# Where operand tiles begin: padded and shifted SBUF tiles in a two-layer encoder trunk

## The chip, the core and the metric

The kernel runs on one NeuronCore of one Trainium2 chip. Five engines work side by side on instruction streams of their own: TensorE (PE in the profile, its weight loads PEld), VectorE (DVE), ScalarE (ACT), GpSimd (POOL) and SyncE (SP, which here issues nearly all DMAs). Operands lie in the on-chip memory SBUF, 128 partitions wide; matmul results go to the accumulators in PSUM. The metric is device time in microseconds (us) of one execution, lower is better.

## The reference

A trunk of two layers on x of 512 tokens x 1024 channels in fp32. Each layer has a token mixer and, beside it, a 4-head cross attention into 256 memory tokens. The mixer of layer 0 is differential attention, that of layer 1 a chunked gated linear attention (GLA). Then comes an output projection, and then a gated MLP with a causal convolution of width 3:

```python
for i in range(DEPTH):                      # DEPTH = 2
    h = rms_norm(x, attn_norm[i])
    proj = h @ w_in                         # (512, 1024) @ (1024, about 2560)
    mix = diff_attention(...) if i % 2 == 0 else gla_attention(...)
    cross = memory_cross_attention(mem_q, mem, ...)
    x = x + concatenate([mix, cross]) @ w_out[i]
    h = rms_norm(x, ffn_norm[i])
    x = x + conv_ffn(h, w_up[i], conv_w[i], conv_b[i], w_down[i])   # width 2816, twice
```

## The kernel before

The residual stream is held transposed: eight tiles xT[k] of 128 channels x 512 tokens. Every large product is made of three matmuls in the format fp32r, because one alone is not exact enough. An fp32 value v is split into a high part, v rounded to fp32r, and a low part, the rest; the product a*b is then ah*bh + ah*bl + al*bh. Helper `split` (L237) makes the pair of an activation: ScalarE writes the high part (L238), VectorE the low part (L239). `split_weights` (L200) does the same for weights (L201 and L204).

Three sorts of SBUF tiles matter here.

- The pool "xs" is a ring of 36 tiles with one tag, 128 partitions x 512 fp32, that is 2048 bytes of each partition. `xtile` (L146) takes one for plain data, `split_tiles` (L149) takes two for a pair of high and low part (names xsh and xsl).
- In the MLP, 5 of the products of each half are kept in xs pairs; the others are kept in a ring of 18 tiles of the same size, tag "mid" (names midh and midl). This ring lies in the pool of the MLP, behind rB, four tiles u of 514 columns each, and six tiles cvo.
- The pool "wp" holds weights: a ring of 3 raw tiles that the DMAs fill, and rings of 5 tiles each for the high and low part (whi and wlo), 1024 columns, 4096 bytes of a partition. One such tile holds a block of a piece of weights: 1024/w rows of 128 input channels, each w columns wide (w is 256, 512 or 272).

`gemm` (L244) makes the input projections: the activation block is the stationary operand, 128 x 128, and the weights are the moving one, up to 512 columns (L255 to L257). `product` (L267) makes the output projection and both MLP products the other way round: 128 columns of weights are stationary, and an activation tile of 512 tokens moves (L272 to L274):

```python
for i in ids:
    (hi, lo), (bh, bl) = parts[i], pairs[i]
    mm(p, hi[:, blk(n)], bh, start=i == first, stop=False)
    mm(p, hi[:, blk(n)], bl, start=False, stop=False)
    mm(p, lo[:, blk(n)], bh, start=False, stop=i == last)
```

The order of TensorE's work is written out by hand: a queue of small units (`Filler`) is drained between the steps of the attention by an estimated cost, so that projections fill the gaps. The other engines' order is set by the tile framework, which also puts in the waits. `weights` (L228) loads and splits the pieces of weights two ahead of their use, in the order of a fixed plan; the load is a DMA of 512 KB on SP's queue (L210).

In the MLP (`ffn`), L1026 to L1060 scale, convolve and gate the result of the up projection and split it again; `update` adds the down projection to xT (L978).

The constants (L161 to L164) lie in one tile C of 768 columns: the identity for transposes, two masks U and BEU in fp32, the same two masks read as integers (MP and MF), and a block of ones. Of the first two nothing reads U and BEU. Small scratch tiles of 16 columns have rings of four by `small` (L154).

Of the kernel before, what the change touches and what calls it, by code (L numbers as in the profile page):

```python
# [11 lines left out]
F32 = mybir.dt.float32  # L12
F32R = mybir.dt.float32r
I32 = mybir.dt.int32
# [7 lines left out]
S = 512  # L22
# [7 lines left out]
WTILE = 1024  # L30
HALVES = (6, 5)
XS = 36
WB = 5
# [96 lines left out]
def trunk(ctx, tc, head_d, x_t, mem_t, wpack, cols_a_d, cols_d, conv_d, gate_d, rel_bias, diff_lambda, consts, onehot, out):  # L130
# [4 lines left out]
    perm = ctx.enter_context(tc.tile_pool(name="perm", bufs=1))  # L135
    xs = ctx.enter_context(tc.tile_pool(name="xs", bufs=1))
    wp = ctx.enter_context(tc.tile_pool(name="wp", bufs=2))
# [5 lines left out]
    def bank(tag):  # L143
        return ps.tile([128, 512], F32, name=f"ps_{tag}", tag=tag)

    def xtile():  # L146
        return xs.tile([128, S], F32, name="xt", tag="xs", bufs=XS)

    def split_tiles(pool=None, tag="xs", bufs=XS):  # L149
        pool = pool or xs  # L150
        return (pool.tile([128, S], F32R, name=tag + "h", tag=tag, bufs=bufs),
                pool.tile([128, S], F32R, name=tag + "l", tag=tag, bufs=bufs))

    def small(name, bufs=None):  # L154
        return cp.tile([128, 16], F32, name=name, tag=name, bufs=bufs)

    def blk(b, w=128):
        return slice(w * b, w * b + w)


    C = perm.tile([128, 768], F32, name="C")  # L161
    ident, U, BEU = C[:, 0:128], C[:, 128:256], C[:, 256:384]
    MP, MF = C[:, 384:512].bitcast(I32), C[:, 512:640].bitcast(I32)
    ones = C[:, 640:768]  # L164
    eps = perm.tile([128, 1], F32, name="eps")
    V.memset(eps, EPS)

# [32 lines left out]
    def split_weights(c, raw, hi, lo, pin=False):  # L200
        ins = A.copy(hi[:, c], raw[:, c])  # L201
        if pin:
            tc.keep_in_program_order(ins)
        V.tensor_sub(lo[:, c], raw[:, c], hi[:, c].bitcast(F32))  # L204

    def raw_tile():
        return wp.tile([128, WTILE], F32, name="raw", tag="raw", bufs=3)

    def load_raw(raw, n):
        nc.sync.dma_start(raw[:, :n], wpack[at[0], :, :n])  # L210
        at[0] += 1
        return raw

    def make_piece(raws=None, between=None):
        parts = []
        for i, (_, _, kk, _, w) in enumerate(blocks[len(made)]):
            n = len(kk)
            raw = load_raw(raw_tile(), n * w) if raws is None else raws[i]
            hi, lo = (wp.tile([128, WTILE], F32R, name=t, tag=t, bufs=WB) for t in ("whi", "wlo"))
            if between is not None and i == 3:  # L220
                between()
            split_weights(slice(0, n * w), raw, hi, lo, len(made) == 2)
            parts += [(hi[:, blk(j, w)], lo[:, blk(j, w)]) for j in range(n)]
        made.append(parts)
# [12 lines left out]
    def split(hi, lo, src, gain):  # L237
        A.activation(hi, src, AF.Copy, scale=gain)  # L238
        V.scalar_tensor_tensor(lo, src, gain, hi.bitcast(F32), op0=ALU.mult, op1=ALU.subtract)  # L239
# [51 lines left out]
    def col(i, t=cols):  # L291
        return t[:, i:i + 1]
# [28 lines left out]
            V.tensor_copy(bs[c.start // 512], p[:6, :n])  # L321

    def lam(lv, lp):
        l2 = small("l2")[:, :2]
        lv4 = lv.rearrange("p (a c b) -> p a c b", a=2, c=2)
        V.tensor_mul(lp, lv4[:, :, 0], lv4[:, :, 1])
        V.reduce_sum(l2, lp, axis=AX.X)
        A.activation(l2, l2, AF.Exp)
        V.scalar_tensor_tensor(nlam, l2[:, 1:2], -LAM_INIT, l2[:, 0:1], op0=ALU.add, op1=ALU.subtract)
# [6 lines left out]
    def squares(src, acc):  # L336
        sq = xtile()
        A.activation(sq, src, AF.Square)
        if acc[0] is not None:
            V.tensor_add(sq, sq, acc[0])  # L340
        acc[0] = sq
# [16 lines left out]
    load = nc.sync.dma_start  # L358
    with tc.tile_pool(name="ini", bufs=1) as ip, tc.manual_schedule(engines={E.Activation, E.DVE, E.Pool, E.SP}):
        idle = ip.tile([128, 512], F32, name="idle")  # L360
        rb = ip.tile([32, 6], F32, name="rb")
        oh = ip.tile([32, 640], F32, name="oh")
        bs = xtile()[:6], xtile()[:6, :128]
        lv = xtile()[:, :256]
        G.memset(idle, 0.0)
        p = bank("tp")
        for n in (512, 320):
            mm(p[:, :n], idle[:, 0:128], idle[:, :n], start=True, stop=True)


        raws = [ip.tile([128, WTILE], F32, name=f"raw{i}") for i in range(4)]
        A.dma_start(raws[0][:, blk(0, S)], wpack[0, :, blk(0, S)])
        head = ip.tile([128, 32 + S], F32, name="head")
        for c in (slice(0, 32 + S // 2), slice(32 + S // 2, 32 + S)):
            load(head[:, c], head_d[:, c])
        xT[0] = head[:, 32:]
        for k in range(1, KT):
            xT[k] = xtile()
            load(xT[k], x_t[k])
            load(raws[k // 2][:, blk(k % 2, S)], wpack[k // 2, :, blk(k % 2, S)])  # L380
        load(cols_a, cols_a_d)
        at[0] = 4
        load(C[:, 640:768], consts[:, 640:768])
        load(rb, rel_bias)
        load(oh, onehot)
        second = [load_raw(raw_tile(), WTILE) for _ in range(3)]
        load(cols, cols_d)
        load(lv, diff_lambda[0].rearrange("a b -> (a b)").partition_broadcast(128))
        parts, acc, split_w = [], [None], [None]
        made.append(parts)  # L390

        def operands(k):
            if k % 2 == 0:
                split_w[0] = [wp.tile([128, WTILE], F32R, name=n, tag=n, bufs=WB) for n in ("whi", "wlo")]
            c = blk(k % 2, S)
            hi, lo = split_w[0]
            xh[k], xl[k] = split_tiles()
            if k == 0:
                V.tensor_copy(hi[:, c], raws[0][:, c])
                V.tensor_sub(lo[:, c], raws[0][:, c], hi[:, c].bitcast(F32))  # L400
                for t in (blk(0, S // 2), blk(1, S // 2)):
                    split(xh[0][:, t], xl[0][:, t], xT[0][:, t], col(0, head))
            else:
                split(xh[k], xl[k], xT[k], col(k, head))
                split_weights(c, raws[k // 2], hi, lo)
            parts.append((hi[:, c], lo[:, c]))
            squares(xT[k], acc)

        operands(0)
        for k in range(KT):  # L410
            if k + 1 < KT:
                operands(k + 1)
            if k == 0:
                second.append(load_raw(raws[0], WTILE))
            if k == 4:
                bias_rows(rb, oh, bs)
            if k == KT - 2:
                make_piece(second, lambda: token_rsqrt("lg", acc[0], NB, r_x[:, 0]))
                weights(("qk", 0))
                small_vectors()  # L420
                for c in range(2):
                    load(bias_d[:, 512 * c:min(512 * c + 512, 640)], bs[c])
            hi, lo = parts[k]
            terms = (xh[k], hi), (xh[k], lo), (xl[k], hi)
            todo = [(b, i) for b in range(NB) for i in range(3)]
            for b, i in sorted(todo, key=lambda bi: bi[1]) if k == 0 else todo:
                xp, w = terms[i]
                mm(first[b], xp[:, blk(b)], w, start=k == 0 and i == 0, stop=k == KT - 1 and i == 2)

    load(C[:, 0:640], consts[:, 0:640])  # L430
    for i in range(4):
        load(memT[i], mem_t[i])
    for l in range(2):
# [294 lines left out]
    def gla_layer(pool, mix, acc):  # L728
# [6 lines left out]
        gl = pool.tile([128, NB, 16], F32, name="gl", bufs=1)  # L735
        gl3, gw3 = split_tiles()
        gl3, gw3 = gl3[:96], gw3[:96, :384]
        rq, rh = small("rq"), small("rh")

        def scales():  # L740
            token_rsqrt("sm", acc[0], NB, r_x[:, 2], True)
# [58 lines left out]
        for h in range(4):  # L800
            pz = bank(("lg", "sm")[h % 2])
            mm(pz[:96], gw3[:, blk(h, 96)], gl3, start=True, stop=True)
            t, la = xtile()[:96], xtile()[:96]
# [291 lines left out]
def _constants():  # L1095
    import numpy as np

    i = np.arange(128)
    same = (i[:, None] // 64) == (i[None, :] // 64)
    le = i[:, None] <= i[None, :]  # L1100
    c = np.zeros((128, 768), np.float32)
    c[:, 0:128] = np.eye(128)
    c[:, 128:256] = same & le
    c[:, 256:384] = same & ~le
    c[:, 384:512] = same & le
    c[:, 512:640] = same & ~le
    c[:, 640:768] = 1.0

    rel = np.arange(640) - 511
    n = np.abs(rel)  # L1110
    large = 8 + sum((n >= t).astype(np.int64) for t in (12, 16, 23, 32, 46, 64, 91))
    bucket = np.where(n < 8, n, large) + np.where(rel > 0, 16, 0)
    onehot = (np.arange(32)[:, None] == bucket[None, :]).astype(np.float32)
    return c, np.ascontiguousarray(onehot[:, ::-1])
# [53 lines left out]
```

## Time and profile before

| | |
|---|---|
| median of 3 runs | 1196.5 us (1195.61 to 1196.85) |
| the profiled execution | 1194.47 us, its span 1192.7 us |
| PE busy | 1179.3 us, 5656 instructions |
| PEld busy | 965.8 us |
| DVE busy | 760.1 us |
| ACT busy | 548.3 us |
| DMA | 117.81 MB, mean 99 GB/s |
| granted TensorE clock | 1.000 |

A row of the timeline gives the start of an instruction (us from the start of the span), how long it was in flight, engine, line, operation, output <- inputs, shape, and, in brackets, the idle time before it. Matmuls are pipelined: each is in flight for longer than the distance from its start to the start of the next, and the end is modelled. The distance of the starts is the cost of a matmul in a dense run, and is called the step here. In the groups, "x96 | 38.0, 396 | 0.0" is the count, the busy time in us, the mean of one in ns, and the idle time before them. A line of the waits gives who waited for whom, the total in us, how often, and the longest.

### The profile page before, as it was taken

Reading aid. Unit: us, or ns where it says so; the run is one execution under the profiler, and the core shown is the slowest. Engines: PE = TensorE matmul, PEld = TensorE weight load, DVE = VectorE, ACT = ScalarE, POOL = GpSimd, SP = SyncE. Lnnn points to the kernel's source line nnn. Section 1 sums busy time; section 2 is a strip of 40 time slices with the busy share of each in tenths; the row PEclk is TensorE's granted clock in tenths of the full one; section 3 lists DMA queues with packets and bytes.
Section 4 is the critical chain, followed back from the end, with each engine's and each line's share of the span. In section 5 each row is a group of like instructions: output and inputs, shape, how many; then the busy total and the mean of one; then the engine's idle time right before and its main releaser. Section 6 shows DMA issues by size and latency. Waiting matters only on the chain.

```text
span 1192.7 us, 14774 instructions
## 1 busy us (share of the span) xinstructions
PE 1179.3 (99%) x5656; PEld 965.8 (81%) x5656; DVE 760.1 (64%) x1270; ACT 548.3 (46%) x966; POOL 4.5 (0%) x25
## 2 busy tenths in 40 slices
PE   9999998999999999999999999999999999999998
PEld 6887776788888888888888788987888888888887
DVE  7566587687767434767556746768777743476741
ACT  6676586564434223434436534436443422243420
POOL 0000000000000000000000000000000000000000
PEclk9999999999999999999999999999999999999999
DMA  8322214042322332322342221333233233242231
GB/s 296 124 96 81 80 55 141 27 136 76 116 96 86 109 107 71 123 71 89 117 144 78 72 71 58 103 104 125 73 109 103 81 114 106 71 124 72 89 115 44
DMA packets 39268, 117.81 MB, mean 99 GB/s; under 512 B 4671, under 2 KB 6520, under 8 KB 39198
## 3 DMA queue, kind: packets, MB, share of 16 engines
q1 hardware_dynamic: 39054, 116.62, 30.5%
q8 instruction: 44, 0.72, 0.3%
q10 hardware_dynamic: 144, 0.26, 0.1%
q14 instruction: 26, 0.21, 0.1%
HBM read 112.65 MB, written 4.21 MB: 98 GB/s over the span
## 4 chain that ended last, share of the span: by engine, by line
PE 93%; DVE 3%; ACT 2%; DMA 1%; issue 1%; SPq 0%; ACTq 0%; DVEq 0%
PE ps_mm L273 8%; PE ps_mm L274 8%; PE ps_mm L272 8%; PE ps_sm L274 7%; PE ps_sm L273 7%; PE ps_sm L272 7%; PE ps_mm L255 5%; PE ps_mm L257 5%; PE ps_mm L256 5%; PE ps_lg L273 3%; PE ps_lg L272 3%; PE ps_lg L274 3%; PE ps_tp L272 3%; PE ps_tp L273 3%; PE ps_tp L274 3%; PE ps_tp L170 2%
## 5 line engine op out<-in xcount | busy, mean ns | idle before, releaser
L201 ACT CAST whi<-raw 128x1024 fp32r<-128x1024 f32 (+4 forms) x212 | 208.5, 985 | 263.9 <-PE ps_tp L273 134.7
L204 DVE TENSOR_TENSOR wlo<-raw,whi 128x1024 fp32r<-128x1024 f32 (+4 forms) x212 | 241.3, 1140 | 117.1 <-ACT whi L201 116.4
L272 PE MATMUL ps_mm<-xsh,whi 128*128 128x512 f32 x446 | 176.4, 396 | 0.0
L273 PE MATMUL ps_mm<-xsl,whi 128*128 128x512 f32 x446 | 173.8, 390 | 0.2 <-DVE xsl L239 0.2
L274 PE MATMUL ps_mm<-xsh,wlo 128*128 128x512 f32 x446 | 173.7, 389 | 0.0
L272 PE MATMUL ps_sm<-xsh,whi 128*128 128x512 f32 x386 | 150.3, 389 | 0.0
L274 PE MATMUL ps_sm<-xsh,wlo 128*128 128x512 f32 x386 | 150.2, 389 | 0.0
L273 PE MATMUL ps_sm<-xsl,whi 128*128 128x512 f32 x386 | 150.2, 389 | 0.0
L255 PE MATMUL ps_mm<-whi,xsh 128*128 128x512 f32 (+2 forms) x352 | 136.9, 389 | 0.1
L257 PE MATMUL ps_mm<-whi,xsl 128*128 128x512 f32 (+2 forms) x352 | 131.1, 373 | 0.3 <-DVE xsl L239 0.3
L256 PE MATMUL ps_mm<-wlo,xsh 128*128 128x512 f32 (+2 forms) x352 | 130.6, 371 | 0.0
L1028 ACT ACTIVATE cvo<-u,cv 128x512 f32<-128x512 f32 x88 | 71.6, 814 | 121.4 <-DVE u L1026 121.4
L273 PEld LDWEIGHTS ps_mm<-xsl,whi 128*128 128x128 f32 x446 | 83.8, 188 | 17.8 <-DVE xsl L239 0.6
L272 PEld LDWEIGHTS ps_mm<-xsh,whi 128*128 128x128 f32 x446 | 83.8, 188 | 17.5 <-issue 0.8
L274 PEld LDWEIGHTS ps_mm<-xsh,wlo 128*128 128x128 f32 x446 | 83.7, 188 | 17.4
L1029 DVE SCALAR_TENSOR_TENSOR cvo<-u,cv,cvo 128x512 f32<-128x512 f32 x88 | 65.8, 748 | 38.7 <-ACT cvo L1028 38.7
L273 PEld LDWEIGHTS ps_sm<-xsl,whi 128*128 128x128 f32 x386 | 72.5, 188 | 15.1
L272 PEld LDWEIGHTS ps_sm<-xsh,whi 128*128 128x128 f32 x386 | 72.5, 188 | 15.0
L274 PEld LDWEIGHTS ps_sm<-xsh,wlo 128*128 128x128 f32 x386 | 72.5, 188 | 15.0
L255 PEld LDWEIGHTS ps_mm<-whi,xsh 128*128 128x128 f32 x352 | 66.3, 188 | 13.8 <-issue 3.4
L257 PEld LDWEIGHTS ps_mm<-whi,xsl 128*128 128x128 f32 x352 | 66.1, 188 | 12.6 <-DVE xsl L239 0.5
L256 PEld LDWEIGHTS ps_mm<-wlo,xsh 128*128 128x128 f32 x352 | 66.4, 189 | 9.7
(257 smaller groups left out, 1734.9 us busy)
## 6 DMA issues: line engine op xcount, KB each, us to landing
raw<-in_wpack_dram SPq DMA_DIRECT2D x178, 512.0 KB, 3.5
xt<-in_x_t_dram SPq DMA_DIRECT2D x15, 256.0 KB, 5.9
raw<-in_wpack_dram SPq DMA_DIRECT2D x15, 256.0 KB, 2.6
raw<-in_wpack_dram SPq DMA_DIRECT2D x8, 384.0 KB, 3.4
xres<-xt SPq DMA_DIRECT2D x8, 256.0 KB, 2.0
xt<-xres SPq DMA_DIRECT2D x8, 256.0 KB, 3.9
out_dram<-xt SPq DMA_DIRECT2D x8, 256.0 KB, 2.0
bt<-bias_d SPq DMA_DIRECT2D x6, 256.0 KB, 3.1
```

The costliest lines, as they stand in the source:

```text
L170: nc.tensor.transpose(dst, src, ident[:n, :n])
L201: ins = A.copy(hi[:, c], raw[:, c])
L204: V.tensor_sub(lo[:, c], raw[:, c], hi[:, c].bitcast(F32))
L255: mm(p, sh[k][:, blk(b)], hi, start=k == 0, stop=False)
L256: mm(p, sh[k][:, blk(b)], lo, start=False, stop=False)
L257: mm(p, sl[k][:, blk(b)], hi, start=False, stop=k == KT - 1)
L272: mm(p, hi[:, blk(n)], bh, start=i == first, stop=False)
L273: mm(p, hi[:, blk(n)], bl, start=False, stop=False)
L274: mm(p, lo[:, blk(n)], bh, start=False, stop=i == last)
L1028: A.activation(c, u[:, 2:], AF.Identity, scale=cv[l][:, 2, j:j + 1], bias=cv[l][:, 3, j:j + 1])
L1029: V.scalar_tensor_tensor(c, u[:, 1:S + 1], cv[l][:, 1, j:j + 1], c, op0=ALU.mult, op1=ALU.add)
```

## The change

The tiles of xs, of mid and of the split weights become longer than what is used of them: 528 columns for 512, and 1032 for 1024. A pair of split tiles is in addition used from column 0, 4, 8 or 12 on, in turn (0, 16, 32 or 48 bytes). Plain x tiles are used from column 0. So the places where the tiles begin, which were all the same modulo 512 bytes within a pool, now differ from tile to tile in steps of 16 bytes. Two unread masks are dropped from the constants, and three small scratch tiles get one buffer instead of four, which makes room for the padding. What is computed, and the order in which PE computes it, stay the same.

```diff
     def xtile():
-        return xs.tile([128, S], F32, name="xt", tag="xs", bufs=XS)
+        return xs.tile([128, S + 16], F32, name="xt", tag="xs", bufs=XS)[:, :S]
+
+    shift = cycle((0, 4, 8, 12))
 
     def split_tiles(pool=None, tag="xs", bufs=XS):
-        pool = pool or xs
-        return (pool.tile([128, S], F32R, name=tag + "h", tag=tag, bufs=bufs),
-                pool.tile([128, S], F32R, name=tag + "l", tag=tag, bufs=bufs))
+        pool, o = pool or xs, next(shift)
+        return (pool.tile([128, S + 16], F32R, name=tag + "h", tag=tag, bufs=bufs)[:, o:o + S],
+                pool.tile([128, S + 16], F32R, name=tag + "l", tag=tag, bufs=bufs)[:, o:o + S])
...
-    C = perm.tile([128, 768], F32, name="C")
-    ident, U, BEU = C[:, 0:128], C[:, 128:256], C[:, 256:384]
-    MP, MF = C[:, 384:512].bitcast(I32), C[:, 512:640].bitcast(I32)
-    ones = C[:, 640:768]
+    C = perm.tile([128, 512], F32, name="C")
+    ident = C[:, 0:128]
+    MP, MF = C[:, 128:256].bitcast(I32), C[:, 256:384].bitcast(I32)
+    ones = C[:, 384:512]
...
-            hi, lo = (wp.tile([128, WTILE], F32R, name=t, tag=t, bufs=WB) for t in ("whi", "wlo"))
+            hi, lo = (wp.tile([128, WTILE + 8], F32R, name=t, tag=t, bufs=WB)[:, :WTILE] for t in ("whi", "wlo"))
...
-        l2 = small("l2")[:, :2]
+        l2 = small("l2", 1)[:, :2]
...
-                split_w[0] = [wp.tile([128, WTILE], F32R, name=n, tag=n, bufs=WB) for n in ("whi", "wlo")]
+                split_w[0] = [wp.tile([128, WTILE + 8], F32R, name=n, tag=n, bufs=WB)[:, :WTILE] for n in ("whi", "wlo")]
...
-    load(C[:, 0:640], consts[:, 0:640])
+    load(C[:, 0:384], consts[:, 0:384])
...
-        rq, rh = small("rq"), small("rh")
+        rq, rh = small("rq", 1), small("rh", 1)
```

More of the change, by code (lines that the diff above doesn't have):

```diff
@@ L382, in trunk @@
         at[0] = 4
-        load(C[:, 640:768], consts[:, 640:768])
+        load(C[:, 384:512], consts[:, 384:512])
         load(rb, rel_bias)
@@ L1100, in _constants @@
     le = i[:, None] <= i[None, :]
-    c = np.zeros((128, 768), np.float32)
+    c = np.zeros((128, 512), np.float32)
     c[:, 0:128] = np.eye(128)
@@ L1104, in _constants @@
     c[:, 256:384] = same & ~le
-    c[:, 384:512] = same & le
-    c[:, 512:640] = same & ~le
-    c[:, 640:768] = 1.0
+    c[:, 384:512] = 1.0
     rel = np.arange(640) - 511
```

## The prediction

> **What bounds the kernel now.** I read the page first, top down: TensorE (PE) has work in flight for 99% of the span, in every slice, at the full granted clock, and the chain that ended last is 93% PE. The other engines have room.
>
> ```profile
> span 1192.7 us, 14774 instructions
> PE 1179.3 (99%) x5656; PEld 965.8 (81%) x5656; DVE 760.1 (64%) x1270; ACT 548.3 (46%) x966; POOL 4.5 (0%) x25
> PEclk9999999999999999999999999999999999999999
> PE 93%; DVE 3%; ACT 2%; DMA 1%; issue 1%; SPq 0%; ACTq 0%; DVEq 0%
> ```
>
> Next the waits of PE. The longest is 2.2 us; all that are listed come to about 9 us, so there is no wait whose removal or lengthening would be the main term.
>
> ```profile
> PE ps_sm L640 <- DVE o L649: 2.2, 1, 2.2
> PE ps_lg L504 <- DVE nmd L609: 1.3, 1, 1.3
> PE ps_lg L604 <- ACT xt L511: 1.1, 3, 0.5
> ```
>
> So the time is the number of matmuls times the time from the start of one to the start of the next, and that step is what I looked for in the timeline. These rows are PE's in the first down projection of layer 0: the first and the last of 24 matmuls whose moving operand is an xsh or xsl tile, then the first ones and the last of 21 with a midh or midl tile, then xsh again.
>
> ```profile
> 388.81 0.39 PE L272 MATMUL ps_sm<-xsh,whi 128*128 128x512 f32 x1
> ...
> 394.02 0.39 PE L274 MATMUL ps_lg<-xsh,wlo 128*128 128x512 f32 x1
> 394.25 0.40 PE L272 MATMUL ps_lg<-midh,whi 128*128 128x512 f32 x1
> 394.48 0.39 PE L273 MATMUL ps_lg<-midl,whi 128*128 128x512 f32 x1
> 394.70 0.40 PE L274 MATMUL ps_lg<-midh,wlo 128*128 128x512 f32 x1
> 394.94 0.39 PE L272 MATMUL ps_lg<-midh,whi 128*128 128x512 f32 x1
> 395.17 0.40 PE L273 MATMUL ps_lg<-midl,whi 128*128 128x512 f32 x1
> ...
> 398.90 0.40 PE L274 MATMUL ps_lg<-midh,wlo 128*128 128x512 f32 x1
> 399.14 0.39 PE L272 MATMUL ps_tp<-xsh,whi 128*128 128x512 f32 x1
> ```
>
> With xs tiles the step is (394.25 - 388.81)/24 = 226.7 ns. With mid tiles it is (399.14 - 394.25)/21 = 232.9 ns, 6.2 ns more, for the same shape, the same weight tiles and the same engine. The groups by form say it over the whole kernel: 395 to 396 ns in flight against 389 to 391.
>
> ```profile
> L273 PE MATMUL ps_lg<-midl,whi 128*128 128x512 f32 x96 | 38.0, 396 | 0.0
> L274 PE MATMUL ps_tp<-midh,wlo 128*128 128x512 f32 x96 | 38.0, 395 | 0.0
> L273 PE MATMUL ps_lg<-xsl,whi 128*128 128x512 f32 x80 | 31.3, 391 | 0.0
> L274 PE MATMUL ps_lg<-xsh,wlo 128*128 128x512 f32 x80 | 31.1, 389 | 0.0
> L274 PE MATMUL ps_sm<-xsh,wlo 128*128 128x512 f32 x386 | 150.2, 389 | 0.0
> ```
>
> What differs is where the tiles begin. In the addresses of the built program every xs, whi and wlo tile begins at 416 modulo 512 bytes, since their sizes (2048 and 4096 bytes) are multiples of 512 and the blocks of weights used within them start 512 bytes apart. The mid tiles lie behind four u tiles of 514 elements (2056 bytes, taking 2080), so they begin 4 x 32 = 128 bytes further on, at 32. While one matmul streams its moving operand, the weights of the next are loaded. I call the distance between these two starts, modulo 512, the phase. Of the 4515 matmuls with 512 fp32r columns, 3931 have phase 0 before the change and 576, those on mid tiles, have phase 128; 8 have others. So the trace already holds a small trial of the change, and there a start out of phase is dearer.
>
> A second sample speaks more mildly. The projection "gm" of layer 1 packs blocks of 272 columns (1088 bytes), so its moving blocks run through phases 0, 64 and 128. From 630.27 to 636.17 there are 47 of them.
>
> ```profile
> 630.27 0.29 PE L256 MATMUL ps_mm<-wlo,xsh 128*128 128x272 f32 x1
> ...
> 636.17 0.40 PE L255 MATMUL ps_mm<-whi,xsh 128*128 128x512 f32 x1
> ```
>
> ```profile
> 760.47 0.28 PE L255 MATMUL ps_mm<-whi,xsh 128*128 128x256 f32 x1
> ...
> 762.50 0.28 PE L257 MATMUL ps_mm<-whi,xsl 128*128 128x256 f32 x1
> ```
>
> The 17 matmuls of 256 columns from 760.47 to 762.50, all in phase, take 119.4 ns each, 120 within the rounding. Against 226.7 ns for 512 columns that is 0.417 ns a column and a fixed 13.3 ns. 272 columns in phase should then take 126.7 ns; the mix of three phases took 5.90/47 = 125.5 ns. So a phase of 64, and 128 on a shorter block, cost nothing there.
>
> **The change part by part.** *Tiles that begin elsewhere.* xs tiles get 528 columns for 512 (a pitch of 2112 bytes, 64 more), mid tiles likewise, each pair of split tiles starts 0, 4, 8 or 12 elements into its tile, and whi and wlo get 1032 columns for 1024 (32 bytes more). In the addresses of the changed program the phases of the same 4515 matmuls spread over all 32 steps of 16 bytes: 92 at 0, 1048 within 64 bytes of 0 on either side, 3467 further out. Before, 584 were further out. No instruction is added, and PE's order is the same in both programs.
>
> The price of a phase that no row shows is bounded by the rows there are. Below: the 272-column mix, -1.2 ns; below even that, nothing excludes that the whole fixed 13.3 ns is a collision at phase 0 and goes. Above: the longest mid matmuls are in flight for 398 ns against 389, 9 ns more, and I let the fixed part double (+13.3 ns) as the outer end, since a half-turn of 256 bytes is in no row.
>
> ```profile
> L272 PE MATMUL ps_lg<-midh,whi x96: 392/395/398, 394.2 to 1181.2; 128*128 128x512 f32 x96
> ```
>
> I take 6.2 ns for a phase beyond 64 bytes, as the mid rows are the only ones of the same shape, 4515 such matmuls being nearly the whole of PE (4515 x 0.2267 = 1024 us of 1192.7), and nothing within 64 bytes, as the 272-column rows show. (3467 - 584) x 6.2 ns = 17.9 us. All of it is on the path: PE is the chain, and there is no idle time on it to take it in. The ends are -3839 x 13.3 ns = -51 us and +51 us for the 3839 matmuls that leave phase 0; by the nearest rows -3839 x 1.2 = -4.6 us and +3839 x 9 = +34.6 us.
>
> By the Trainium skill, "TensorE: Matmul & The Clock Gate", section "Step-by-step: what each phase is for", TensorE has two independent SBUF read ports, one for the streaming operand and one for LDWEIGHTS. By that the two streams would not meet and this term would be 0. The trace does not agree: 232.9 against 226.7 ns with nothing else changed. It stands below as a rival.
>
> *VectorE and ScalarE on the same tiles.* They read and write the moved tiles. L1060 does the same subtraction into mid tiles (32) and xs tiles (416):
>
> ```profile
> L1060 DVE TENSOR_TENSOR midl<-cvo,midh x24: 683/692/693, 331.4 to 1139.1; 128x512 fp32r<-128x512 f32 x24
> L1060 DVE TENSOR_TENSOR xsl<-cvo,xsh x20: 682/685/693, 279.1 to 1086.5; 128x512 fp32r<-128x512 f32 x20
> ```
>
> The medians differ by 1%. Taken over VectorE's 760 us it would be 7 us on an engine that is idle for 36%, under PE's work: 0. Where that cover is thin, at the splits that PE waits for, it is 7 ns each. The range takes it in.
>
> *Smaller constants and shorter rings of small tiles.* The load of C shrinks from 640 to 384 columns (320 to 192 KB), the doubled masks U and BEU go, MP and MF move within C; l2, rq and rh get one buffer where each is made once. Nobody in PE's list of waits waits for C, and a DMA moved past the gate loads on SP's queue changes no listed wait: 0. If C's arrival did hold the first transposes, the gain would be under 1 us.
>
> ```profile
> C<-in_consts_dram SPq DMA_DIRECT2D x1, 320.0 KB
> ```
>
> *DMAs of the moved tiles.* Each partition still gets one run of 2048 bytes; the transfers that refill xs tiles land in 3.9 us and are asked for well before their use. The last store (2.0 us) is on the path and starts at a 32-byte multiple as before: 0, at most some tenths of a us.
>
> ```profile
> xt<-xres SPq DMA_DIRECT2D x8, 256.0 KB, 3.9
> out_dram<-xt SPq DMA_DIRECT2D x8, 256.0 KB, 2.0
> ```
>
> **The sum.** The profiled execution took 1194.5 us (span 1192.7 and 1.8 around it), 2.0 below the median of 1196.5. 1194.5 + 17.9 = 1212.4, and on the scale of the median 1214.4. I say 1214.
>
> **The rivals.** *Faster: phase 0 is itself the collision.* All tiles at one place mean that the moving stream and the weight load go through the same part of each 512 bytes in step, and the fixed 13.3 ns may be what that costs. Spread phases would then lose less on the mean. For it: the 272-column mix is 1.2 ns under what phase 0 gives, and one mid matmul took only 0.22 us (394.48 to 394.70). Against it: the mid tiles as a whole. By the 272-column price it is 1196.5 - 4.6 = 1192; with a quarter of the fixed part gone, 3839 x 3.3 ns = 12.8 us, 1184; with all of it, 1145. It decides from the point where the mean over the phases falls under the 226.7 ns of phase 0.
>
> *No change: the places don't matter.* The mid matmuls would be slow for another cause of their own place in the memory, not for the phase, or the gains of some phases pay for the losses of others. 1196.5. This is also where the two read ports of the skill's page lead. Against it: the step returns to 0.23 us and under as soon as xs tiles are back, and all other loads of the stage are the same.
>
> *Much slower: jumps cost more than a fixed phase.* Mid tiles keep one phase from matmul to matmul; after the change nearly every matmul starts at another. If each of 3839 then pays the 9 ns of the slow mid matmuls, 1196.5 + 34.6 = 1231; at double the fixed part, 1248. For it: the few matmuls after the return to xs tiles are still slow (0.40 us in the row below, 0.39 in phase).
>
> ```profile
> 399.37 0.40 PE L273 MATMUL ps_tp<-xsl,whi 128*128 128x512 f32 x1
> 399.84 0.40 PE L272 MATMUL ps_tp<-xsh,whi 128*128 128x512 f32 x1
> ```
>
> **How the numbers follow.** A measurement of this kernel tells a difference from about 0.2% (2.4 us) on. Slower by a price near that of the mid rows, 1203 to 1226: 0.48. Much slower: 0.19. Faster: 0.27, of which some 0.08 below 1182. No change: 0.06. So slower 0.67, same 0.06, faster 0.27. The range leaves out what lies over 1240 (0.08) and under 1182 (0.08). The likeliest case alone is 1203 to 1226.
>
> **What would show it.** Right: the groups of 512-column matmuls on xs tiles rise from 389 to about 394 ns, the step from 226.7 to 231 ns or so, evenly in all stages and not in one; PE's waits stay as short as they are; VectorE's and ScalarE's means stay within 1%. The runs on mid tiles, whose phases now vary as well, would no longer stand out against their neighbours. Wrong: a mean under 389 ns on xs tiles (phase 0 was the collision), or PE waits for DVE or ACT that grow by more than 2 us in all (the moved tiles slow the other engines), or a difference of time with an unchanged step.

## The result, and the profile after

The changed kernel takes 1210.7 us (median of 4 runs, 1209.6 to 1212.1) against 1196.7 us before: 14.0 us more, ratio 1.0126 with a 95% interval of 1.0113 to 1.0138. The forecast was 1214, slower with a chance of 0.67.

The page of the profiled execution after the change; its span of 1210.3 us belongs to a run of 1212.1 us, so the spans differ by 17.6 us where the medians differ by 14.0. The second line is busy time by engine, the last the chain that ended last.

```profile
span 1210.3 us, 14771 instructions
PE 1196.6 (99%) x5656; PEld 968.0 (80%) x5656; DVE 760.7 (63%) x1270; ACT 547.5 (45%) x966; POOL 4.5 (0%) x25
PEclk9999999999999999999999999999999999999999
PE 90%; DVE 4%; ACT 3%; DMA 2%; issue 1%; SPq 0%; ACTq 0%; DVEq 0%
```

The same 5656 records keep TensorE busy for 17.3 us longer, at the same clock; VectorE and ScalarE do their work in the same time as before (760.7 and 547.5 us against 760.1 and 548.3). The waits of PE are the same ones; of what is new, the longest is 0.4 us:

```profile
PE ps_sm L642 <- DVE o L651: 2.2, 1, 2.2
PE ps_lg L506 <- DVE nmd L611: 1.3, 1, 1.3
PE ps_mm L257 <- ACT ks L559: 0.4, 1, 0.4
```

The groups by form after the change, columns as in the prediction (the lines have moved by 2):

```profile
L275 PE MATMUL ps_lg<-midl,whi 128*128 128x512 f32 x96 | 38.0, 396 | 0.0
L276 PE MATMUL ps_sm<-xsh,wlo 128*128 128x512 f32 x386 | 151.9, 394 | 0.0
```

Every group of 512 columns with an xs tile as its moving operand has gained 2 to 6 ns in flight, the one shown from 389 to 394; the mid groups have stayed or lost up to 2 ns, and no longer stand out. The timeline of the same down projection gives the step: 41 matmuls on xs tiles from 392.66 to 402.13 us take 231.0 ns each (226.7 before), the 15 on mid tiles from there to 405.61 take 232.0 (232.9 before).

```profile
392.66 0.39 PE L275 MATMUL ps_sm<-xsl,whi 128*128 128x512 f32 x1
...
402.13 0.40 PE L274 MATMUL ps_lg<-midh,whi 128*128 128x512 f32 x1
...
405.61 0.39 PE L274 MATMUL ps_lg<-midh,whi 128*128 128x512 f32 x1
```

So nothing waits for longer; it is the matmuls that have become a little slower. The distances from one start to the next, added up over both traces, say where the time went: behind the projections' 960 matmuls of 512 columns 228.2 us before and 232.3 after, behind the products on xs tiles 679.7 and 693.9, on mid tiles 134.6 and 133.6, behind all others 144.8 and 145.0. That is 17.3 us for the large matmuls and 0.2 us for the rest.

### The profile page after: what moved, and what is told of

The parts are those of the page before. It is cut to its first block, busy times and chain, and to the rows that moved or that the text cites. A ratio compares the mean times of both kernels' runs of the same rounds, so it can differ in the third digit from the quotient of the medians.

```text
span 1210.3 us, 14771 instructions
## 1 busy us (share of the span) xinstructions
PE 1196.6 (99%) x5656; PEld 968.0 (80%) x5656; DVE 760.7 (63%) x1270; ACT 547.5 (45%) x966; POOL 4.5 (0%) x25
## 4 chain that ended last, share of the span: by engine, by line
PE 90%; DVE 4%; ACT 3%; DMA 2%; issue 1%; SPq 0%; ACTq 0%; DVEq 0%
PE ps_mm L275 8%; PE ps_mm L276 8%; PE ps_mm L274 8%; PE ps_sm L274 7%; PE ps_sm L276 7%; PE ps_sm L275 7%; PE ps_mm L257 5%; PE ps_mm L259 5%; PE ps_mm L258 5%; PE ps_lg L275 3%; PE ps_lg L276 3%; PE ps_lg L274 3%; PE ps_tp L274 3%; PE ps_tp L275 3%; PE ps_tp L276 3%; PE ps_tp L172 2%
```

## The experiments

Three explanations were open. The phase theory: the step depends on where the moving operand begins against the weights. The hop theory: a constant place costs little, but a place that changes from matmul to matmul does. And: it is other engines, or the place in the memory, that make matmuls slow.

### The matmuls alone, phase by phase

```python
for a, b, n in steps:      # a: start of the moving operand, b: of the weights, n: columns
    nc.tensor.matmul(p[i % 4][:, :n], st[:, b:b + 128], mv[:, a:a + n], start=True, stop=True)
    i += 1
```

> The kernel's work is left out: nothing but fp32r matmuls on one 128x2048 moving and one 128x1024 stationary tile, in runs of 36 or 72, with no other engine at work, so that TensorE's own two streams are alone. Runs paa to pdh hold one phase each (start of the moving operand less start of the weights that are being loaded, modulo 512 bytes), from 0 to 496 bytes in steps of 16. ba and bb move both operands by 128 and 256 bytes (phase 0), ca and cb the weights alone. da hops to another phase with every matmul, db, dc and dd change between 0 and 128, 256 and 64 bytes, de hops in steps of 64, df hops with the weights in steps of 32. ea and eb repeat one pair of operands at phase 0 and 128. ga to gd are 256 and 384 columns at 0 and 128. Phase theory: 226.7 ns at 0, 233 at 128 (run pba), other phases between 224 and 238, ba and bb 226.7, ca and cb as the phases 384 and 256. Hop theory: every steady phase is near 226.7, and da, de are at 231 to 232. If the mid tiles were slow for their place in the memory or for other engines, all runs are at 226.7.

In the timeline of PE equal instructions are merged, so each run of matmuls is a row, and the distance of two starts over 36 (or 72) is the mean step. Runs pab to pbh are the phases 16 to 240, pca to pch the phases 256 to 368.

```profile
20.18 8.50 PE L61 MATMUL pab<-mv,st 128*128 128x512 f32 x36
28.51 8.57 PE L61 MATMUL pac<-mv,st 128*128 128x512 f32 x36
36.92 8.55 PE L61 MATMUL pad<-mv,st 128*128 128x512 f32 x36
...
78.61 8.53 PE L61 MATMUL pba<-mv,st 128*128 128x512 f32 x36
86.97 8.55 PE L61 MATMUL pbb<-mv,st 128*128 128x512 f32 x36
...
137.42 8.33 PE L61 MATMUL pbh<-mv,st 128*128 128x512 f32 x36
145.58 8.36 PE L61 MATMUL pca<-mv,st 128*128 128x512 f32 x36
153.78 8.50 PE L61 MATMUL pcb<-mv,st 128*128 128x512 f32 x36
162.12 8.57 PE L61 MATMUL pcc<-mv,st 128*128 128x512 f32 x36
...
279.19 8.38 PE L61 MATMUL ba<-mv,st 128*128 128x512 f32 x36
287.40 8.33 PE L61 MATMUL bb<-mv,st 128*128 128x512 f32 x36
295.57 8.53 PE L61 MATMUL ca<-mv,st 128*128 128x512 f32 x36
303.94 8.32 PE L61 MATMUL cb<-mv,st 128*128 128x512 f32 x36
312.10 16.88 PE L61 MATMUL da<-mv,st 128*128 128x512 f32 x72
328.81 16.72 PE L61 MATMUL db<-mv,st 128*128 128x512 f32 x72
345.38 16.50 PE L61 MATMUL dc<-mv,st 128*128 128x512 f32 x72
361.72 16.80 PE L61 MATMUL dd<-mv,st 128*128 128x512 f32 x72
```

From these rows: 231.4 ns at phase 16, 233.6 at 32, 232.2 at 128 (pba); rows left out here give 229.2 at 64 and 234.2 at 160. At 240 (that is -16) it is 226.7, as good as in phase. At 256 it is (153.78 - 145.58)/36 = 227.8, with the run's first matmuls still slow; then the curve repeats: 231.7 at 272 against 231.4 at 16. The period is 256 bytes and not 512. From 145.58 to 279.19, one whole turn of 256 bytes, 576 matmuls take 232.0 ns each. Moving both operands costs nothing (bb: 226.9), moving the weights alone costs the same as moving the other operand (ca: 232.5, cb by 256: 226.7). Hops over all phases give 232.1 (da), hops of 0 and 256 bytes 226.9 (dc). So hops over all phases cost what constant phases cost on the mean, and nothing more. Hops between 0 and 64 bytes do cost more: 231.0 (dd, with the start of the run after it), where the mean of the two phases is 228.0. TensorE does all this to itself, as no other engine was at work. No phase is clearly below 226.7 ns.

### The mid ring in phase

```diff
-        us = [pool.tile([128, S + 2], F32, name=f"u{i}", bufs=1) for i in range(4)]
+        us = [pool.tile([128, S + 26], F32, name=f"u{i}", bufs=1)[:, :S + 2] for i in range(4)]
```

> The kernel before with the four u tiles padded to 538 columns, so that the mid ring begins 4 x 128 bytes later and is at 416 modulo 512 like all other operands. Phase theory: the mid groups fall from 395 to about 390 ns in flight, the step from 232.9 to 226.7 ns, 576 x 6.2 ns = 3.6 us, so 1193.1 us. If the mid tiles are slow because of where in the memory they lie: 1196.7, no change.

Measured: 1192.8 us against 1196.8, ratio 0.9966 (0.9954 to 0.9979). The groups by form of this run:

```profile
L273 PE MATMUL ps_lg<-midl,whi 128*128 128x512 f32 x96 | 37.6, 391 | 0.2
L274 PE MATMUL ps_tp<-midh,wlo 128*128 128x512 f32 x96 | 37.3, 389 | 0.0
L274 PE MATMUL ps_lg<-xsh,wlo 128*128 128x512 f32 x80 | 31.1, 389 | 0.0
```

The mid tiles are as fast as the xs tiles as soon as they are in phase, though they lie in the same part of the memory as before but for 384 bytes (each u tile has grown by 96 bytes, not by the 128 of the expectation). This is also a kernel faster than both, by an edit of one line.

### A constant gap, 128 and 256 bytes

```diff
+    gap = ctx.enter_context(tc.tile_pool(name="gap", bufs=1)).tile([128, 32], F32, name="gap")   # 64 for xs256
+    G.memset(gap, 0.0)
     wp = ctx.enter_context(tc.tile_pool(name="wp", bufs=2))
```

> The kernel before with a gap of 128 bytes between the xs ring and the weights: all tiles of a ring keep one place modulo 512, but xs against weights is 128 or 384 bytes out of phase for nearly all matmuls, and nothing hops. Phase theory: 3900 x 6.2 ns = 24 us more, 1221. Hop theory (what costs is that the place changes from matmul to matmul): 1197 to 1200.

> The kernel before with a gap of 256 bytes between the xs ring and the weights: 3898 of 4515 matmuls at phase 256, 37 at 0, the mid tiles still at 128. By the first scan, in which 256 is as good as 0, the time stays: 1196.8. If in the kernel it is the distance modulo 512 that counts, or any distance, it is as with the gap of 128 bytes: 1213.

Measured: with 128 bytes 1213.3 us, ratio 1.0135 (1.0119 to 1.0150); with 256 bytes 1195.5 us, ratio 0.9996 (0.9986 to 1.0005). One row of the groups of each, first of the gap of 128 and then of 256 bytes:

```profile
L276 PE MATMUL ps_sm<-xsh,wlo 128*128 128x512 f32 x386 | 152.3, 394 | 0.0
```

```profile
L276 PE MATMUL ps_sm<-xsh,wlo 128*128 128x512 f32 x386 | 150.2, 389 | 0.0
```

The hop theory falls: with nothing hopping, a constant 128 bytes lose 16.5 us, more than the whole change. The 1221 expected was 8 us too much, as the price is not 6.2 ns for all: by the traces of before and of this run (distances of starts, without those over 300 ns, which hold gaps) the projections' step rises from 229.0 to 232.6 ns and that of the products on xs tiles from 227.1 to 232.4. The period of 256 bytes holds in the kernel as well.

### Each padding alone

The changed kernel with one of its two paddings undone, the constants left as changed:

```diff
# wp_alone
-        return xs.tile([128, S + 16], F32, name="xt", tag="xs", bufs=XS)[:, :S]
+        return xs.tile([128, S], F32, name="xt", tag="xs", bufs=XS)
... (split_tiles likewise, without the shift)
# xs_alone
-            hi, lo = (wp.tile([128, WTILE + 8], F32R, name=t, tag=t, bufs=WB)[:, :WTILE] for t in ("whi", "wlo"))
+            hi, lo = (wp.tile([128, WTILE], F32R, name=t, tag=t, bufs=WB)[:, :WTILE] for t in ("whi", "wlo"))
... (split_w[0] likewise)
```

> The changed kernel with xs and mid tiles as before: only the whi and wlo tiles are padded by 32 bytes, and the constants stay small. The moving operand hops much less, 512 matmuls are in phase. Phase theory: about (4515 - 512 - 584)/(3931 - 92) of the loss of 14 us, so 12 to 13 us, 1209. Hop theory: the place of the moving operand changes seldom in the MLP and only weights hop, a small part of the loss, 1198 to 1202.

> The changed kernel without the padding of the weights: xs and mid tiles padded and shifted, whi and wlo as before. The phases are spread as widely as in the changed kernel. By the first scan's table the loss is that of the whole change within 0.3 us, 1210; if the two paddings added up, it would be the rest of the weights' part, 1197 to 1198.

Measured: the weights' padding alone 1210.6 us, ratio 1.0117 (1.0103 to 1.0130); the padding and shift of xs and mid alone 1211.2 us, ratio 1.0121 (1.0106 to 1.0136). Either half costs what the whole costs: once the phases are spread, spreading them further does no more harm. Both runs keep the smaller constants and the shorter rings, so they can't tell what these bring; no run here has them alone. The traces before and after leave them little room: all that is not a matmul of 512 columns on split operands changed by 0.2 us.

### What the phase acts on

> The kernel's work is left out, as in the first scan: matmuls alone. a and z are phase 0 with 128 columns of weights (226.7 ns expected). ha, hb, hc load 96, 64 and 32 columns of weights at phase 0, ia, ib, ic the same at phase 128. If the fixed 13.3 ns is what the weight load takes from the moving stream, it falls with the columns, to 10, 6.7 and 3.3 ns (223, 220, 217), and the loss at phase 128 falls likewise; if it is the change of weights itself, it stays 226.7. qa to qg are phases of 4, 8, 12, 16, 20, 24 and 32 bytes, ra to rg the same with the weights ahead (phases -4 to -32): a rule by 16-byte lines gives 226.7 up to a line's width on one side or both, one by exact places loses at 4 bytes already. na is in phase with the weights that are being loaded but 128 bytes off those in use, nb the other way round: if the load is what the moving stream meets, na is 226.7 and nb near 232. ka, kb use 64 partitions. ma, mb, mc are bf16 at 0, 32 and 128 bytes: half the bytes for a column, so little or no loss.

The timeline of PE, as above:

```profile
28.60 8.44 PE L63 MATMUL ha<-mv,st 128*96 128x512 f32 x36
36.88 8.49 PE L63 MATMUL ia<-mv,st 128*96 128x512 f32 x36
...
78.45 8.74 PE L63 MATMUL qa<-mv,st 128*128 128x512 f32 x36
87.02 8.52 PE L63 MATMUL ra<-mv,st 128*128 128x512 f32 x36
...
136.96 8.56 PE L63 MATMUL rd<-mv,st 128*128 128x512 f32 x36
145.36 8.56 PE L63 MATMUL qe<-mv,st 128*128 128x512 f32 x36
...
195.71 16.72 PE L63 MATMUL na<-mv,st 128*128 128x512 f32 x72
212.27 16.61 PE L63 MATMUL nb<-mv,st 128*128 128x512 f32 x72
228.82 8.51 PE L63 MATMUL ka<-mv,st 64*128 64x512 f32 x36
...
253.44 7.93 PE L63 MATMUL mb<-mb,sb 128*128 128x512 bf16 x36
261.21 7.93 PE L63 MATMUL mc<-mb,sb 128*128 128x512 bf16 x36
```

In bf16 the place doesn't matter: (261.21 - 253.44)/36 = 215.8 ns at 32 bytes, and 216.1 in phase (ma, whose row is left out). In fp32r a start 4 bytes off costs the most of all that were tried (qa: 238.1). Loading fewer columns of weights in phase doesn't make the step shorter but longer (ha: 230.0 with 96 columns; with 64, whose row is left out, 230.0 too), so the explanation that each line of weights takes its time from the moving stream falls. At 128 bytes 96 columns take 231.4 (ia), so there the phase costs only 1.4 ns. With 64 partitions the loss stays: 226.7 in phase once the run ka has settled, 235.8 at 128 bytes (kb, whose row is left out). With weights that change between 0 and 128 bytes, neither a moving operand in phase with the next weights (na: 230.0) nor one in phase with those in use (nb: (16.61 - 0.39)/71 = 228.5) is at 226.7; this doesn't tell which of the two it meets. And rd, 64 against 80 bytes, a distance of -16, is at 233.3, where 240 against 0 was at 226.7: the distance is not all that counts.

### Other engines beside the matmuls

VectorE and ScalarE got some 130 us of additions and copies of their own, at the matmuls' place modulo 256 bytes and 128 bytes on.

> The kernel's work is left out: 936 matmuls at phase 0 on TensorE, and beside them VectorE and ScalarE at work on tiles of their own, one kind of operation after the other: additions of two SBUF tiles, additions with PSUM, ScalarE copies, both engines at once, first at the same place modulo 256 bytes as the matmuls' tiles, then 128 bytes on. The matmuls wait for none of it. If TensorE's two streams meet only each other, every step is 226.7 ns. If the other engines' reads and writes of SBUF meet them as well, the step rises while they work, by up to the 5 ns that some matmuls of the kernel before show beside VectorE.

```profile
29.63 110.55 PE L66 MATMUL a<-mv,st 128*128 128x512 f32 x487
```

(110.55 - 0.39)/486 = 226.7 ns over 487 matmuls, through all kinds of work beside them. The Trainium skill says so, in "SBUF — State Buffer", section "SBUF: two separate sides": PE never waits on the other engines' ports. Here it agrees. The matmuls on xs tiles that are slow in the kernel before, in the groups ps_lg and ps_tp at 390 and 391 ns, follow the mid tiles. In the run mid0, which moves the mid tiles alone, these groups are at 389, with VectorE's work as it was.

### The other operands of TensorE in phase

```diff
+    eps = perm.tile([128, 1], F32, name="eps")       # moved ahead of C
     C = perm.tile([128, 768], F32, name="C")
...
-    nlam = perm.tile([128, 1], F32, name="nlam")
+    nlam = perm.tile([128, 25], F32, name="nlam")[:, 0:1]
... (r_mem and kd padded likewise, on top of mid0)
```

> As the run mid0, and in addition the other tiles that TensorE reads are put at the same place modulo 256 bytes as xs and the weights: the constants with the identity, kmT and vm, and the GLA state tiles. In the scans a run of matmuls at phase 0 needs some ten matmuls after an interruption before its steps are 226.7 ns, at a cost of about 45 ns. If it is the place of the interrupting operands that breaks the lock, the projections between the small matmuls of the attention get back part of their 229 ns against 226.7, up to 2 us: 1191 to 1192. If any interruption breaks it, the time is that of mid0, 1192.8.

> The kernel of the run mid0 once more, beside all0 on the same chip: 1192.8, 0.3 to 0.4% under the kernel before.

Measured: 1192.4 us, ratio 0.9973 (0.9964 to 0.9983), and for mid0 beside it 1192.5 us, ratio 0.9968 (0.9957 to 0.9978). The same within the noise, and the projections' step is 228.9 ns in both traces: moving the interrupting operands gained nothing that can be seen.

## Why the prediction was right, and where its steps were off

**The bound** held: PE is the chain, its waits did not grow, and a price on each matmul went into the time almost whole (17.3 of the 17.6 us between the two spans).

**The mechanism** held: the phase between the moving operand and the weights. The run with the mid ring in phase and the two gaps show it in the kernel, the scan shows it for TensorE alone. That it counts modulo 256 and not 512 bytes does not change the sign, since in the scan 14 of 16 places lose all the same. (Of the two that don't, -16 bytes is shown only with weights at 0; with the weights at 80 bytes it was at 233.3 ns.)

**The size** was off in three terms, two of which partly cancel. The price of 6.2 ns was read from one phase; the mean over a turn is 232.0 - 226.7 = 5.3 ns. And "nothing within 64 bytes", taken from the 272-column rows, is the step that failed: in the scan 16 bytes cost 4.7 ns and 32 cost 6.9, only -16 nothing; those rows were of shorter matmuls, and at 256 columns the scan too finds 128 bytes no dearer than phase 0 (118.6 against 119.4 ns):

```profile
428.26 4.46 PE L61 MATMUL ga<-mv,st 128*128 128x256 f32 x36
432.56 4.43 PE L61 MATMUL gb<-mv,st 128*128 128x256 f32 x36
436.83 6.41 PE L61 MATMUL gc<-mv,st 128*128 128x384 f32 x36
```

With the scan's step for each phase, the phases of the two programs make 23.6 us after and 3.0 before, 20.6 us of difference, against the 17.9 of the prediction; measured are 14.0. The third term is the step before, 226.7 ns, which the prediction took from one dense stretch of products for all 3931 matmuls in phase. By the trace of before (again without distances over 300 ns) the products on xs tiles are at 227.1 ns and the projections, which run in the attention with small matmuls between them, at 229.0. After the change they are at 231.6 and 232.0, near the scan's mean of 232.0. So the projections lose 3.0 ns and not 5.3: 888 x 2.3 + 2945 x 0.4 = 3.2 us of the 20.6 had been paid before. This brings the sum near the 17.3 us that the two traces differ by in these matmuls; the remaining 3.3 us to 14.0 is that the profiled runs lie further apart than the medians. That the forecast of 1214 came within 4 us of 1210.7 is in part luck: the right price for each phase, with the step of 226.7 kept, would have given 1217.

In the groups, the projections' first matmul of three (L255) rises from 409 to 412 ns, the other two from 390 and 391 to 394, most groups of the products from 389 to 394. The first of these groups, before and then after the change:

```profile
L255 PE MATMUL ps_mm<-whi,xsh 128*128 128x512 f32 x288 | 117.9, 409 | 0.0
```

```profile
L257 PE MATMUL ps_mm<-whi,xsh 128*128 128x512 f32 x288 | 118.7, 412 | 0.4 <-ACT ks L559 0.4
```

In the scans a run in phase begins, after an interruption, with up to some ten steps between 224 and 236 ns before it settles at 226.7 (the run ba does). That this settling is what holds the projections at 229.0 is argued and not shown; no run here takes the interruptions away.

**The other edits** at nothing: they were not run alone, but no wait of PE is new by more than 0.4 us, and all but the large matmuls changed by 0.2 us. VectorE's and ScalarE's work on shifted tiles: right, L1062 after the change has 691 and 686 ns where L1060 had 692 and 685.

**The rivals.** *Phase 0 is itself the collision* falls: no phase of the scan is clearly under it at 512 columns. *No change* falls; the two independent read ports of the Trainium skill ("TensorE: Matmul & The Clock Gate", "Step-by-step: what each phase is for") fit the bf16 runs, where places don't matter, and not fp32r. *Jumps cost more* falls for jumps over all phases: 232.1 ns for hops, 232.0 for the mean of constant phases; only the hops between 0 and 64 bytes cost 3 ns more than their two phases.

**Open:** what in TensorE's reading of fp32r operands makes the phase count, whether the stream meets the weights being loaded or those in use, why fewer columns of weights are slower, and why a stream in phase takes some matmuls to settle.

## What to carry to other kernels

Where fp32r matmuls bound a kernel, put the start of every moving operand and of every block of weights at one place modulo 256 bytes of a partition; here it was worth up to 5 ns of 232 for each 512-column matmul, and a tile of odd size ahead of a pool is enough to lose it. A group of equal matmuls that is some per cent slower than its neighbours in the groups by form is a sign of it. Padding tiles so that their places differ spreads nothing that collides here; it takes the matmuls out of step.

## What the runs showed that was not expected

- The period is 256 bytes (256 bytes of gap: 0.9996 of the time; 128: 1.0135), and -16 bytes is as good as 0 when the weights begin at 0.
- The step of an fp32r matmul of 512 columns can take some ten matmuls after an interruption to settle. In bf16 it is 215.8 ns at once, 10.9 ns less than the best of fp32r.
- The dearest place of those tried is 4 bytes off: 238.1 ns.
- Fewer columns of weights make the step longer: 230.0 ns for 96 or 64 against 226.7 for 128.
- With a work of their own on SBUF and PSUM, VectorE and ScalarE slowed 487 matmuls by nothing measurable.
